# Four edits to the projection of a hybrid attention/recurrence layer: PSUM banks, product order, one engine swap, and a fixed VectorE order

## The chip, the cores and the metric

The kernel runs on one core of a Trainium2 chip. The metric is the device time of one execution in microseconds (us); lower is better. TensorE is called PE, VectorE DVE, ScalarE ACT, GpSimd POOL, and SyncE (which issues the DMAs) SP.

## The reference

One decoder layer on x of shape (1, 1024, 2048), float32:

```
h    = rms_norm(x, norm_gain)
proj = h @ w_in                      # 2048 x 6144: q, k, v, attention gate, recurrent input, recurrent gate
o    = diff_attention(rope(q), rope(k), v, lam)        # 8 heads, two score maps a head, causal
o    = rms_norm(o, subln_gain) * (1 - lam_init) * silu(g_attn)
r    = rg_lru(causal_conv(xr)) * silu(g_rec)           # 8 blocks of 128 channels
out  = rms_norm(x + concat(o, r) @ w_out, final_gain)
...
log_a = -8 * r * softplus(-lru_lambda);  a = exp(log_a)
mult  = sqrt(-expm1(2 * log_a))                        # = sqrt(1 - a*a)
```

## The kernel before

**Products.** All matmuls keep float32 accuracy by splitting each operand into a high and a low part (`hi`, `lo`): three matmuls for one product. The projection is cut into 48 "pairs" of output columns; a pair takes seven block products of a fast matrix scheme (numbers `pi` 0 to 6, 12 matmuls each) over one half (k = 0 or 1) of the contraction. The 48 pairs run in three segments: segment 0 has 8 recurrent pairs of k = 0 (their results go to memory as partials), segment 1 has 16 attention pairs and 8 recurrent pairs of k = 1, segment 2 has the 16 attention pairs of k = 0. In segment 1 the recurrent pairs are finished and `recurrent` follows; in segment 2 the attention pairs are finished and `rope` or `values` follows.

**Banks.** A pair writes its products into four PSUM banks by name, `BANKS = ("al", "de", "be", "al", "ga", "be", "ga")` for `pi` 0 to 6. `post` reads them: after product 0 ACT copies `al`; after 1 DVE makes result 11 from `de`; after 3 ACT copies `al` (L552, called u2) and DVE adds `be` (u3); after 4, 5 and 6 DVE makes results 22, 21 and 12. There are two sets of banks: `pp` (set 0) and `pq` (set 1). The first two pairs of a segment, and the last two of segments 0 and 1, run side by side with one set each; all other pairs run one after another, overlapped, on set 0 alone (`chained`). Of set 1, `al` and `be` also take the small matmuls of `recurrent` and `values`.

**Order.** `projection` writes out the list of products. At each it first writes `prep` of the product three places ahead (for `pi` 2, 3 and 6 a DVE subtraction or two, then `split`; for 4 `split` alone), then the 12 matmuls, then `post`. `split` (L188) is a cast on ACT to `hi` and then a subtraction for `lo`, on DVE, or on POOL for `pi` 0, 1 and 5. Other work (`recurrent`, `rope`, `values`, `scores`, `weighted`) is written as generators that a hand-made clock (`Slots`) advances by four ticks a product, with `yield n` as a delay of n ticks. The order written so is a priority only: the compiler's scheduler orders the instructions of each engine by its own model of when each can start. On the chip each engine then runs its list in that fixed order.

**Later stages.** `rec_half` multiplies the recurrent half by `w_out` (L1097 to L1099) while attention runs (`score` L873 to L910, `unturn` L1018 to L1027). `att_half` then multiplies the attention half; before each of its two row blocks, `att_mix` splits eight operands (cast on ACT, subtraction on DVE), and at its end `finish_row` normalizes.

Of the kernel before, what the change touches and what calls it, by code (L numbers as in the profile page):

```python
# [13 lines left out]
F32 = mybir.dt.float32  # L14
# [3 lines left out]
AF = mybir.ActivationFunctionType  # L18
ALU = mybir.AluOpType
AX = mybir.AxisListType  # L20

P = 128
# [5 lines left out]
NR = 8  # L28
# [25 lines left out]
BANKS = ("al", "de", "be", "al", "ga", "be", "ga")  # L54
# [51 lines left out]
class Pair:  # L106
# [3 lines left out]
    def __init__(self, k, us, done=None, key=None):  # L110
        self.k = k
        self.us = us
        self.done = done
        self.key = key
        self.s = 0
        self.x = {}
        self.w = {}
        self.c = {}
        self.p = {}


class Trunk:
# [86 lines left out]
    def consts2(self):  # L209
        nc, cst, io = self.nc, self.cst, self.io  # L210
        make_identity(nc, self.ident)
        nc.gpsimd.memset(self.mask, 0.0)
        nc.gpsimd.affine_select(
            out=self.mask, in_=self.mask, pattern=[[-1, MASKW]], base=896,
            channel_multiplier=1, compare_op=ALU.is_ge, fill=NEG)
        self.subg = cst.tile([P, 1], F32, name="subg")
        nc.vector.tensor_scalar_mul(self.subg, self.vec[:, VSG:VSG + 1], 0.5 * (1.0 - LAM_INIT))
        b1, b2 = self.alloc(), self.alloc()
        lv = b1.f[:, :4 * QK]
        nc.sync.dma_start(lv, io["lamv"].broadcast_to([P, 4 * QK]))  # L220
        yield 8
        lv = lv.rearrange("p (a b) -> p a b", a=4)
        pr = b2.f[:, :2 * QK].rearrange("p (a b) -> p a b", a=2)
        nc.vector.tensor_tensor(out=pr, in0=lv[:, 0:4:2, :], in1=lv[:, 1:4:2, :], op=ALU.mult)
        sm = cst.tile([P, 2], F32, name="lvs")
        nc.vector.reduce_sum(sm, pr, axis=AX.X)
        self.rel(b1, b2)
        nc.scalar.activation(sm, sm, AF.Exp)
        yield 1
        self.lam = cst.tile([P, 1], F32, name="lam")  # L230
        nc.vector.tensor_tensor(out=self.lam, in0=sm[:, 0:1], in1=sm[:, 1:2], op=ALU.subtract)
        nc.vector.tensor_scalar_add(self.lam, self.lam, LAM_INIT)
        self.nlam = cst.tile([P, 1], F32, name="nlam")
        nc.vector.tensor_scalar_mul(self.nlam, self.lam, -1.0)
        ll = self.vec[:, VLL:VLL + NR]
        t = [cst.tile([P, NR], F32, name=f"sp{i}") for i in range(5)]
        nc.vector.tensor_scalar_mul(t[0], ll, -1.0)
        nc.vector.tensor_tensor(out=t[1], in0=t[0], in1=ll, op=ALU.max)
        nc.scalar.activation(t[1], t[1], AF.Exp, scale=-1.0)
        yield 1  # L240
        nc.vector.tensor_scalar_add(t[2], t[1], 2.0)
        nc.vector.reciprocal(t[2], t[2])
        nc.vector.tensor_tensor(out=t[1], in0=t[1], in1=t[2], op=ALU.mult)
        nc.vector.tensor_tensor(out=t[2], in0=t[1], in1=t[1], op=ALU.mult)
        nc.vector.memset(t[3], 1.0 / 17)
        for k in (15, 13, 11, 9, 7, 5, 3, 1):
            nc.vector.tensor_tensor(out=t[3], in0=t[3], in1=t[2], op=ALU.mult)
            nc.vector.tensor_scalar_add(t[3], t[3], 1.0 / k)
            yield 1
        nc.vector.tensor_tensor(out=t[3], in0=t[3], in1=t[1], op=ALU.mult)  # L250
        nc.vector.tensor_scalar_max(t[4], t[0], 0.0)
        nc.vector.tensor_scalar_mul(t[3], t[3], 2.0)
        nc.vector.tensor_tensor(out=t[4], in0=t[4], in1=t[3], op=ALU.add)
        self.nsp = cst.tile([P, NR], F32, name="nsp")
        nc.vector.tensor_scalar_mul(self.nsp, t[4], -8.0)

# [279 lines left out]
    def partial(self, pr, name):  # L538
        p = pr.p[name] = self.alloc()
        self.load(p.f, self.part[pr.key, name])  # L540

    def post(self, pr, pi):
        nc, b = self.nc, self.bank[pr.s]
        if pi == 0:
            pr.a1 = self.alloc()
            nc.scalar.copy(pr.a1.f, b["al"])
        elif pi == 1:
            self.result(pr, "11", b["de"], pr.a1)
            self.rel(pr.a1)
        elif pi == 3:  # L550
            pr.u2, pr.u3 = self.alloc(), self.alloc()
            nc.scalar.copy(pr.u2.f, b["al"])  # L552
            self.tt(pr.u3.f, b["be"], pr.u2.f, ALU.add)
        elif pi == 4:
            self.result(pr, "22", b["ga"], pr.u3)
            self.rel(pr.u3)
        elif pi == 5:
            self.result(pr, "21", b["be"], pr.u2)
        elif pi == 6:
            self.result(pr, "12", b["ga"], pr.u2)  # L560
            self.rel(pr.u2)
            if pr.done:
                self.after.append(self.sl.spawn(pr.done(pr.c), 1))

    def chained(self, pairs):


        q = [(pairs[0], pi) for pi in range(3)]
        for n, p in enumerate(pairs):
            q += [(p, 3), (p, 4)]  # L570
            for pi in (5, 6):
                if p is not pairs[-1]:
                    q.append((pairs[n + 1], pi - 5))
                q.append((p, pi))
            if p is not pairs[-1]:
                q.append((pairs[n + 1], 2))
        return q

    def projection(self):
        nc, sl = self.nc, self.sl  # L580
# [12 lines left out]
        q, starts, ends, dualp = [], [], [], set()  # L593
# [51 lines left out]
        for i, (p, pi) in enumerate(q):  # L645
            seg = max(s for s in range(3) if starts[s] <= i)
            if i in starts:
                if i == 0:
                    sl.spawn(self.consts2(), 60)
                    sl.spawn(self.squares(sl.spawn(self.second_operands(), 60)), 64)  # L650
                if seg == 1:
                    sl.spawn(self.rope_tables(), 60)
            if seg < 2 and i == ends[seg] - 15:
                sl.spawn(self.operands(1 - seg))
            for x in loads.get(i, ()):
                self.raw(*x)
            for x in parts.get(i, ()):
                self.partial(*x)
            for op in first.pop(i, ()) if seg == 0 else ():
                self.first_operand(op)  # L660
            if i + LEAD < len(q):
                self.prep(*q[i + LEAD])
            if OPS[pi] not in self.Y:
                while len(self.Ynext.get(OPS[pi], ())) < 4:
                    sl.tick()
                self.Y[OPS[pi]] = self.Ynext.pop(OPS[pi])
            dual = p in dualp
            while dual and not self.dual and self.side:
                sl.tick()
            self.dual = dual  # L670
            acc = self.bank[p.s][BANKS[pi]]
            hi, lo = p.w.pop(pi)
            for qq in range(4):
                yh, yl = self.Y[OPS[pi]][qq]
                s = slice(qq * P, (qq + 1) * P)
                for j, (a, b) in enumerate(((hi, yh), (hi, yl), (lo, yh))):
                    nc.tensor.matmul(acc, lhsT=a.r[:, s], rhs=b.r,  # L677
                                     start=FIRST[pi] and qq == 0 and j == 0,
                                     stop=qq == 3 and j == 2, skip_group_check=True)
                sl.tick()  # L680
            self.rel(hi, lo)
            self.post(p, pi)
            if last[seg, pi] == i:
                for hl in self.Y.pop(OPS[pi]):
                    self.rel(*hl)
            if seg == 2 and i >= ends[2] - 7:
                self.out_prefetch(i - ends[2] + 7)
# [15 lines left out]
    def recurrent(self, n, c4):  # L703
        nc, v = self.nc, self.vec
# [48 lines left out]
                yield 2  # L753
            self.rel(ch[l], cl[l])
        self.rel(gw)
        sp = self.nsp[:, n:n + 1]
        th = [self.alloc(), self.alloc()]
        a = [self.alloc(), self.alloc()]
        for l in range(2):
            nc.scalar.activation(th[l].f, gates[l, 0].f, AF.Tanh, scale=sp)  # L760
        for l in range(2):
            nc.scalar.activation(a[l].f, gates[l, 0].f, AF.Exp, scale=sp)
            self.tt(gates[l, 1].f, gates[l, 1].f, cs[l].f, ALU.mult, nc.gpsimd)
            self.rel(cs[l])
            yield 1
        for l in range(2):
            r = gates[l, 0]
            self.tt(r.f, a[l].f, a[l].f, ALU.mult, nc.gpsimd)
            yield 3
            nc.vector.scalar_tensor_tensor(out=r.f, in0=r.f, scalar=1.0, in1=th[l].f,  # L770
                                           op0=ALU.add, op1=ALU.mult)
            yield 1
# [412 lines left out]
            self.rel(y)  # L1185

    def run(self):
        if True:
            self.consts()
            self.projection()  # L1190
            self.rec_half()
            self.att_half()
# [61 lines left out]
```

## Time and profile before

| | |
|---|---|
| median of 3 runs | 1716.01 us (1712.44 to 1718.68) |
| profiled execution | 1710.78 us |
| its span, first to last instruction | 1709.0 us |
| mean granted PE clock | 0.972 |

Most executions of one kernel agree within 0.3%. The busy share of an engine is a mean over stages with different limits; the stages are told apart below by time from the start of the span: the first 214 us hold segment 0, 214 to about 725 us segment 1, to about 1101 us segment 2, 1117 to 1510 us attention beside the first half of the output projection, and the rest the second half.

### The profile page before, as it was taken

How to read it: one execution, taken by the hardware profiler on the slowest of the kernel's cores; microseconds unless marked ns; L12 is line 12 of the kernel's file. 1: busy time of each engine (PE TensorE's matmuls, PEld its weight loads, DVE VectorE, ACT ScalarE, POOL GpSimd, SP SyncE). 2: the span in 40 equal slices, each digit the busy share in tenths (PEclk: the TensorE clock that was granted, in tenths of full speed). 3: DMA queues.
4: the chain of work that ended last, by engine and by line, in shares of the span. 5: the costliest groups of instructions: out<-in, count | busy, mean ns of one | idle time of the engine just before them, and what ended most of it. 6: DMA issues, size and time to landing. Idle time of an engine off the chain costs nothing. (4 is left out here: it accounts for less than half of the span.)

```text
span 1709.0 us, 22289 instructions
## 1 busy us (share of the span) xinstructions
PE 1561.2 (91%) x7140; PEld 1265.1 (74%) x7140; DVE 1278.1 (75%) x2120; ACT 816.4 (48%) x1462; POOL 615.7 (36%) x486
## 2 busy tenths in 40 slices
PE   6977998998999899998998998889999999989997
PEld 4765876787777777877777777767777777868786
DVE  8856759777987889889999988857777777761412
ACT  6443633645456355653323333335665555663432
POOL 3474421424334234451222222324222322357370
PEclk9998999999999999999999999999999999999999
DMA  6665732433424332575665555877577655474642
GB/s 253 223 219 182 240 119 82 130 95 110 131 79 135 120 120 96 196 237 181 205 198 185 183 181 167 298 287 272 177 228 246 209 164 165 147 249 134 223 153 99
DMA packets 168277, 304.18 MB, mean 178 GB/s; under 512 B 19040, under 2 KB 21216, under 8 KB 168160
## 3 DMA queue, kind: packets, MB, share of 16 engines
q1 hardware_dynamic: 168160, 302.76, 53.3%
q8 instruction: 56, 0.92, 0.2%
q14 instruction: 61, 0.50, 0.1%
HBM read 206.22 MB, written 96.47 MB: 177 GB/s over the span
## 5 line engine op out<-in xcount | busy, mean ns | idle before, releaser
L677 PE MATMUL pp<-b,b 128*128 128x512 f32 x3612 | 881.8, 402 | 96.8 <-ACT b L552 49.5
L677 PEld LDWEIGHTS pp<-b,b 128*128 128x128 f32 x3612 | 696.9, 194 | 263.7 <-ACT b L552 57.5
L190 POOL TENSOR_TENSOR b<-b,b 128x512 fp32r<-128x512 f32 x288 | 429.4, 1504 | 779.8 <-ACT b L189 458.1
L189 ACT CAST b<-b 128x512 fp32r<-128x512 f32 x592 | 353.3, 619 | 526.7 <-DVE b L193 202.1
L190 DVE TENSOR_TENSOR b<-b,b 128x512 fp32r<-128x512 f32 x304 | 234.2, 785 | 74.9 <-ACT b L189 52.5
L193 DVE TENSOR_TENSOR b<-b,b 128x512 f32<-128x512 f32 x340 | 269.7, 809 | 18.0 <-DMA b<-w_in 6.3
L1099 PE MATMUL pq<-b,b 128*128 128x512 f32 x512 | 203.3, 397 | 3.6 <-DVE b L190 3.6
L1098 PE MATMUL pq<-b,b 128*128 128x512 f32 x512 | 203.6, 398 | 1.6 <-POOL b L190 1.6
L1097 PE MATMUL pq<-b,b 128*128 128x512 f32 x512 | 203.0, 397 | 0.0
L193 DVE TENSOR_TENSOR b<-pp,b 128x512 f32<-128x512 f32 x215 | 146.1, 680 | 39.3 <-ACT b L552 22.0
L193 DVE TENSOR_TENSOR b<-pq,b 128x512 f32<-128x512 f32 x89 | 61.0, 686 | 108.4 <-PE pq L1099 102.0
L900 ACT ACTIVATE wide<-sw,mx 128x256 f32<-128x256 f32 (+7 forms) x128 | 93.9, 739 | 61.7 <-DVE mx L896 60.4
L193 POOL TENSOR_TENSOR b<-b,b 128x512 f32<-128x512 f32 (+1 forms) x56 | 82.1, 1469 | 106.1 <-DVE b L699 38.3
L1099 PEld LDWEIGHTS pq<-b,b 128*128 128x128 f32 x512 | 96.7, 189 | 21.4 <-DVE b L190 5.4
L193 DVE TENSOR_TENSOR b<-b,wide 128x512 f32<-128x512 f32 x120 | 104.5, 884 | 9.7 <-ACT wide L1167 9.1
L893 DVE CUSTOM_DVE_ANT_0 sw<-sw,mask 128x256 f32<-128x256 f32 (+7 forms) x128 | 96.7, 762 | 17.9 <-PE sw L889 16.4
L1098 PEld LDWEIGHTS pq<-b,b 128*128 128x128 f32 x512 | 96.8, 189 | 17.5 <-POOL b L190 2.0
L1097 PEld LDWEIGHTS pq<-b,b 128*128 128x128 f32 x512 | 96.8, 189 | 15.9
L677 PE MATMUL pq<-b,b 128*128 128x512 f32 x420 | 104.6, 395 | 2.3 <-POOL b L190 1.0
L677 PEld LDWEIGHTS pq<-b,b 128*128 128x128 f32 x420 | 80.1, 191 | 20.3 <-POOL b L190 1.4
L1024 ACT CAST b<-pq 128x512 fp32r<-128x512 f32 (+1 forms) x80 | 43.5, 544 | 76.7 <-PE pq L1015 73.7
L888 PE MATMUL sw<-b,b 128*128 128x512 f32 (+2 forms) x192 | 70.9, 372 | 9.0 <-ACT wide L900 8.7
(149 smaller groups left out, 1574.6 us busy)
## 6 DMA issues: line engine op xcount, KB each, us to landing
b<-w_in SPq DMA_DIRECT2D x192, 256.0 KB, 2.9
b<-w_out SPq DMA_DIRECT2D x128, 256.0 KB, 4.3
pt<-b SPq DMA_DIRECT2D x96, 256.0 KB, 2.7
b<-pt SPq DMA_DIRECT2D x96, 256.0 KB, 2.9
b<-fs SPq DMA_DIRECT2D x96, 256.0 KB, 4.5
b<-xt SPq DMA_DIRECT2D x72, 256.0 KB, 3.9
fs<-b SPq DMA_DIRECT2D x64, 256.0 KB, 2.4
b<-yd SPq DMA_DIRECT2D x32, 256.0 KB, 4.6
```

The lines of the kernel that those rows point to most:

```text
L189: self.nc.scalar.copy(hi.r, x)
L190: (eng or self.nc.vector).tensor_tensor(out=lo.r, in0=x, in1=hi.f, op=ALU.subtract)
L193: (eng or self.nc.vector).tensor_tensor(out=out, in0=a, in1=b, op=op)
L677: nc.tensor.matmul(acc, lhsT=a.r[:, s], rhs=b.r, start=FIRST[pi] and qq == 0 and j == 0, stop=qq == 3 and j == 2, skip_group_check=True)
L888: nc.tensor.matmul(o, lhsT=q[m].r[:, qs], rhs=kk, start=True, stop=False)
L893: nc.vector.tensor_tensor_reduce(out=s, in0=s, in1=self.mask[:, 896 - off:896 - off + cols], scale=1.0, scalar=NEG, op0=ALU.add, op1=ALU.m ...
L900: nc.scalar.activation(p[:, :cols], self.swide[m][:, :cols], AF.Exp, scale=QK ** -0.5, bias=mx[:, m:m + 1], accum_out=sm[:, m:m + 1])
L1024: nc.scalar.copy(wh.r[:, first:], self.tr[:, first:])
L1097: nc.tensor.matmul(acc, lhsT=mh.r[:, s], rhs=wh.r, start=kt == 0, stop=False)
L1098: nc.tensor.matmul(acc, lhsT=mh.r[:, s], rhs=wl.r, start=False, stop=False)
L1099: nc.tensor.matmul(acc, lhsT=ml.r[:, s], rhs=wh.r, start=False, stop=kt == 7)
```

## The change

1. **Banks.** Each second chained pair (`odd`) takes banks `ga` and `de` of set 1 in place of `al` and `be` of set 0; `ga` and `de` of set 0 stay shared by all.
2. **Order.** Products of pair p and the next pair n were written 3p 4p 0n 5p 1n 6p 2n; they are written 3p 4p 0n 1n 5p 6p 2n.
3. **Square.** In `recurrent`, a*a was a POOL multiplication of `a` by itself with a delay of 3 ticks behind it; ACT now makes it as a second Exp of the same input with a doubled scale (`nsp2`), and the delay goes.
4. **DVE order.** The scheduler keeps all DVE instructions in the order in which the program writes them. The other engines are still ordered by the scheduler.

```diff
+        self.nsp2 = cst.tile([P, NR], F32, name="nsp2")
+        nc.vector.tensor_scalar_mul(self.nsp2, t[4], -16.0)
...
+    def banks(self, pr):
+        b = self.bank[pr.s]
+        if pr.odd:
+            b = {**b, "al": self.bank[1]["ga"], "be": self.bank[1]["de"]}
+        return b
+
     def post(self, pr, pi):
-        nc, b = self.nc, self.bank[pr.s]
+        nc, b = self.nc, self.banks(pr)
...
         for n, p in enumerate(pairs):
+            p.odd = n % 2
+            nxt = pairs[n + 1] if p is not pairs[-1] else None
             q += [(p, 3), (p, 4)]
-            for pi in (5, 6):
-                if p is not pairs[-1]:
-                    q.append((pairs[n + 1], pi - 5))
-                q.append((p, pi))
-            if p is not pairs[-1]:
-                q.append((pairs[n + 1], 2))
+            if nxt:
+                q += [(nxt, 0), (nxt, 1)]
+            q += [(p, 5), (p, 6)]
+            if nxt:
+                q.append((nxt, 2))
...
-            acc = self.bank[p.s][BANKS[pi]]
+            acc = self.banks(p)[BANKS[pi]]
...
             nc.scalar.activation(a[l].f, gates[l, 0].f, AF.Exp, scale=sp)
+            nc.scalar.activation(gates[l, 0].f, gates[l, 0].f, AF.Exp, scale=sp2)
...
             r = gates[l, 0]
-            self.tt(r.f, a[l].f, a[l].f, ALU.mult, nc.gpsimd)
-            yield 3
...
     def run(self):
-        if True:
+        with self.tc.manual_schedule(engines={mybir.EngineType.DVE}):
```

## Rows read from the trace of the kernel before

**Rows 1.** The page: busy us, share of the span, instructions of each engine.

```profile
PE 1561.2 (91%) x7140; PEld 1265.1 (74%) x7140; DVE 1278.1 (75%) x2120; ACT 816.4 (48%) x1462; POOL 615.7 (36%) x486
```

**Rows 2.** Stretches: length; busy us (instructions) of each engine; PE clock; DMA share; GB/s.

```profile
85.00:214.00 129.00, 108.78 (x451) 87.60 (x450) 82.86 (x100) 62.63 (x108) 72.29 (x50) 0.93 0.65 213
...
171.00:214.00 43.00, 43.00 (x191) 35.63 (x190) 31.40 (x45) 26.02 (x46) 20.77 (x14) 1.00 0.70 238
...
214.00:725.00 511.00, 473.52 (x2006) 385.35 (x2006) 418.69 (x564) 261.72 (x396) 181.06 (x123) 0.97 0.36 117
...
787.00:1101.00 314.00, 283.93 (x1211) 228.17 (x1210) 291.41 (x416) 107.64 (x187) 78.83 (x47) 0.96 0.62 203
...
1117.00:1510.00 393.00, 367.57 (x2056) 300.79 (x2054) 289.53 (x735) 228.18 (x471) 113.44 (x140) 0.99 0.62 208
```

**Rows 3.** What PE waited for: us in total, times, longest.

```profile
PE pp L677 <- ACT b L552: 49.5, 17, 6.1
PE pp L677 <- DVE b L193: 28.6, 13, 5.4
```

**Rows 4.** What DVE waited for, 787 to 1101 us: total, times, longest.

```profile
DVE b L190 <- ACT b L189: 19.2, 5, 4.6
```

**Rows 5.** The same, 214 to 725 us.

```profile
DVE b L770 <- POOL b L193: 22.5, 6, 7.6
```

**Rows 6.** DVE instructions by form, 787 to 1101 us: busy us, mean ns, idle before.

```profile
L193 DVE TENSOR_TENSOR b<-b,b 128x512 f32<-128x512 f32 x140 | 107.7, 787 | 2.6 <-issue 1.8
L193 DVE TENSOR_TENSOR b<-b,wide 128x512 f32<-128x512 f32 x89 | 79.0, 905 | 0.4
L190 DVE TENSOR_TENSOR b<-b,b 128x512 fp32r<-128x512 f32 x87 | 63.3, 729 | 19.3 <-ACT b L189 19.2
```

**Rows 7.** Timeline around 920 us: start, us, engine, instruction [idle before].

```profile
919.12 0.68 DVE L193 TENSOR_TENSOR b<-b,b 128x512 f32<-128x512 f32 x1
...
919.73 0.68 DVE L193 TENSOR_TENSOR b<-b,wide 128x512 f32<-128x512 f32 x1
919.84 0.62 ACT L189 CAST b<-b 128x512 fp32r<-128x512 f32 x1 [0.58 <-DVE b L193]
920.33 0.68 DVE L193 TENSOR_TENSOR b<-b,b 128x512 f32<-128x512 f32 x1
...
920.93 0.68 DVE L190 TENSOR_TENSOR b<-b,b 128x512 fp32r<-128x512 f32 x1
```

**Rows 8.** Timeline around 308 us, the square and its reader.

```profile
308.17 1.04 POOL L193 TENSOR_TENSOR b<-b 128x512 f32<-128x512 f32 x1 [1.84 <-ACT b L762]
...
309.25 0.69 DVE L770 SCALAR_TENSOR_TENSOR b<-b,b 128x512 f32<-128x512 f32 x1 [6.99 <-POOL b L193]
```

**Rows 9.** Line 193 on DVE: ns minimum/median/maximum by where the inputs lie.

```profile
L193 DVE TENSOR_TENSOR b<-b,b x340: 622/680/1790, 19.2 to 1105.0; 128x512 f32<-128x512 f32 x170
L193 DVE TENSOR_TENSOR b<-pp,b x215: 621/679/693, 23.6 to 1103.2; 128x512 f32<-128x512 f32 x108
```

**Rows 10.** Groups by line: the Exp on ACT, the square on POOL.

```profile
L193 POOL TENSOR_TENSOR b<-b 128x512 f32<-128x512 f32 x16 | 17.0, 1073 | 15.2 <-ACT b L762 8.9 <-ACT b L760 6.2
...
L762 ACT ACTIVATE b<-b,nsp 128x512 f32<-128x512 f32 x16 | 11.6, 722 | 0.1
```

**Rows 11.** Groups by line in attention: Exp of the scores, cast in `unturn`.

```profile
L900 ACT ACTIVATE wide<-sw,mx 128x256 f32<-128x256 f32 (+7 forms) x128 | 93.9, 739 | 61.7 <-DVE mx L896 60.4
...
L900 ACT ACTIVATION_READ_ACCUMULATOR wide<-sw,mx 128x1 f32 x128 | 25.3, 197 | 0.0
...
L1024 ACT CAST b<-pq 128x512 fp32r<-128x512 f32 (+1 forms) x80 | 43.5, 544 | 76.7 <-PE pq L1015 73.7
```

**Rows 12.** DVE timeline at the seam of the last stage's row blocks.

```profile
1605.19 0.69 DVE L190 TENSOR_TENSOR b<-b,b 128x512 fp32r<-128x512 f32 x1 [1.28 <-ACT b L189]
...
1611.05 0.69 DVE L193 TENSOR_TENSOR b<-pq,b 128x512 f32<-128x512 f32 x1 [0.41 <-PE pq L1099]
...
1616.85 0.16 DVE L1178 RECIPROCAL yrs<-yrs 128x1 f32<-128x1 f32 x1 [0.36 <-ACT yrs L1177]
```

More of the change, by code (lines that the diff above doesn't have):

```diff
@@ L119, in __init__ @@
         self.p = {}
+        self.odd = 0
 class Trunk:
@@ L755, in recurrent @@
         self.rel(gw)
-        sp = self.nsp[:, n:n + 1]
+        sp, sp2 = self.nsp[:, n:n + 1], self.nsp2[:, n:n + 1]
         th = [self.alloc(), self.alloc()]
```

## The prediction

> **What bounds the kernel now.** I read the busy line of the page first [rows 1]: PE 91%, DVE 75%. That is an average, so next the stretches [rows 2]. In the projection one stretch shows what PE can do: from 171 to 214 us it ran 191 matmuls in 43.0 us without a gap, 0.225 us each. A pair of seven products is 84 matmuls, 18.9 us. Against this stand three other pictures. From 85 to 214 us PE was busy 108.8 of 129 us at a mean clock of 0.93; from 214 to 725 us 473.5 of 511 at 0.97; from 787 to 1101 us 283.9 of 314 at 0.96. A mean below 1 says that part of the stretch ran at the lower of the two levels, 1.2 in place of 2.4 GHz. In these three stretches PE was idle 20.2, 37.5 and 30.1 us, and the clock shortfall times the length is another 9, 15 and 13 us.
>
> Then I asked what PE waited for [rows 3]. The largest wait is for L552, the ACT copy of bank `al` after product 3: 49.5 us in 17 waits. Product 0 of the next pair writes that same bank, with one product (12 matmuls, 2.7 us) between. The second is for DVE's L193, 28.6 us. So PE's gaps are bank gaps, and the first edit goes for the larger.
>
> The last question is whether the engine behind PE could keep up if those gaps closed. From 787 to 1101 us DVE was busy 291.4 us of 314, 93% [rows 2]: this stage is as much DVE's as PE's. Nearly all that DVE idled there, 19.2 us in 5 waits, was for the cast of `split` [rows 4]. From 214 to 725 us DVE was busy 418.7 of 511, 82% [rows 2], and its largest wait was for the POOL square, 22.5 us in 6 [rows 5]. In attention PE was busy 367.6 of 393 us and DVE 289.5 [rows 2].
>
> **Banks and order.** With its own `al` and `be`, an odd pair's product 0 no longer waits for L552, nor its product 2 for result 21. What is late next is u3, which product 5 needs: with the wider order three products (8.1 us) lie between product 3 and product 5 where there were two. The longest wait for L552 was 6.1 us behind one product [rows 3], so the copy may come 8.8 us after product 3 and still hold up product 5 by about 1.4 us at worst. Shared `ga` keeps its distance: two products between 6 and the next pair's 4. The most the two edits can return is all idle and clock of the three stretches, 20+37+30+9+15+13 = 124 us; the waits for L552 alone are 49.5 us.
>
> The Trainium skill (Perfetto Trace Analysis, Matmuls) says that independent matmul groups should rotate through different PSUM banks, so that one's evacuation overlaps the next one's matmuls. The wait for L552 bears that out; what it gives is a rival below.
>
> **Square.** ACT gains 16 Exp of 722 ns, 11.6 us; POOL loses 16 products of 1073 ns, 17.0 us [rows 10]. ACT is busy 262 of 511 us there [rows 2], so the cover is its idle time; without it, 11.6 us. One example: the square took 1.04 us and its reader on DVE had idled 6.99 us, started 0.04 us after the square's end [rows 8]. The new path is shorter by about 1073 - 722 = 351 ns a half. The dropped ticks and the one extra constant cost nothing that shows beside 48 pairs.
>
> **DVE in the written order.** This is the dear part. In `split`, DVE's subtraction needs ACT's cast, and in `prep` (2, 3 and 6) and `rope` the cast needs the DVE instruction written just before. A piece of the timeline shows the length of that round trip and how it is paid now [rows 7]: a DVE instruction started at 919.12 us, the cast at 919.84 for 0.62, and the subtraction could have started at 920.49 or so. DVE did not stand: it started other instructions at 919.73 and 920.33, and its next subtraction came at 920.93. Kept in written order, nothing can step in, and DVE stands from 919.73 to 920.49, 0.76 us. I count these pairs per stage:
>
> - *787 to 1101 us.* A head has two pairs: 2 x 17 DVE instructions of `prep` and `post`, 16 of `rope`, 8 of `values`: 58. The 416 there [rows 2] are 7.2 heads. A head holds 2 x 3 + 4 = 10 such chains, and two more in `values`, where the subtraction waits for a cast of PE's transposes: 12, or 86 in the stretch. 86 x 0.76 = 65 us, of which 19 are paid now [rows 4]: +46. Some comes back, because a standing DVE does not collide with POOL. Line 193 with both inputs in SBUF takes 622 to 1790 ns, with one from PSUM 621 to 693 [rows 9]; over a median of 680, the three SBUF groups hold (107 x 140 + 225 x 89 + 49 x 87) ns = 39 us of excess [rows 6]. DVE would stand 65 of 356 us, 18%, so I take 7 us of it back: **+39**. Bounds: +7, if all 39 us of excess go; and +46, if none does.
> - *214 to 725 us.* 24 pairs give 72 chains, 55 us; the 16 convolution splits 12; and eight times some 2 us for the first reader of the squares: it is written 2 ticks (1.35 us) behind the Tanh, while ACT needs four activations of 722 ns first [rows 10]. DVE then needs 418.7 + 55 + 12 + 16 = 502 us, less some 10 of collisions. PE needs 24 x 18.9 + 96 x 0.225 = 476 (the last term for `recurrent`'s own matmuls). Both are below the 511 of now, so here the banks may win 19; two engines so near each other do not both run full, and I give half of it back: **-10**. Bounds: -35 (PE's 476), and +26, if half of the 70 us that DVE idles there for other things than the square stays on top of the chains.
> - *85 to 214 us.* 24 chains, 18 us, fit into DVE's 46 idle us [rows 2]. PE has 29 us to win at most, and DMA and POOL, 65% and 56% busy, stay: **-8**, between -20 and +5.
> - *Attention, 64 scores in 393 us, 6.14 each.* DVE is busy 4.52 us a score. Between its maximum and its `es` lie two Exp with their reads, 2 x (739 + 197) = 1.87 us [rows 11], with one instruction of some 0.65 us written in between: 1.2 us of standing; and 1.25 `unturn` a score with a cast of 544 ns [rows 11], half of them early: 0.35. That is 6.07 us, just under 6.14; with no cast early and nothing in between 7.1, or +60 in all. I take **+10**, between 0 and +60.
> - *The last stage's seam.* Now all eight subtractions of the second block's `att_mix` run before the first block's last result (1605.19 against 1611.05). In written order they follow `finish_row`, whose reciprocal came at 1616.85 [rows 12]. PE, which read on at once, would wait some 5 us: **+5**, between +3 and +9.
>
> The Trainium skill (SBUF — State Buffer, Who interferes with whom) has a DVE instruction with two SBUF inputs and a POOL instruction that reads SBUF exclude each other. The spread of line 193 agrees with it; by that rule, with every collision moved into a stand, this stage costs the +7 and the sum is 1715, against 1747 by the rows.
>
> **Sum.** 39 - 10 - 8 + 10 + 5 = +36 us on the profiled 1710.8: 1747. The runs' median is 5 us above that execution, so I put it at **1748**.
>
> **The rivals.**
> - *Banks win* (faster). If DVE's stands cost no more than now in 787 to 1101 us (+7), attention pays nothing, and segments 0 and 1 get most of what the banks can give (-18 and -32): 7 - 18 - 32 + 3 = -40, 1671. For it: the 49.5 us wait is PE's largest and surely goes; the order that is replaced was made from a model, and it lets DVE stand 6.99 us for a POOL product [rows 8]. Against it: the 93% of DVE. It decides if DVE's idle time in 787 to 1101 us stays under 25 us. Chance 0.36. By the rule on banks of the Trainium skill (Perfetto Trace Analysis, Matmuls) the result would be this one.
> - *No change.* The chains cost 20 us and the banks give 20: 1711 to 1721 by either count. Chance 0.09.
> - *Attention breaks too* (much slower). The score chain, not PE, sets its 393 us: +60, with +46 in segment 2, nothing in the two others and +5 at the seam: 1711 + 111 = 1822. For it: 1.55 us a score is all the standing that there is room for. Against it: the output matmuls can fill PE. Chance 0.13.
>
> **How the numbers follow.** My forecast, slower by 15 to 70 us, has 0.42. Within 0.3% (5 us) is about what a measurement of this kernel can tell from no change. Slower is 0.42 + 0.13 = 0.55, same 0.09, faster 0.36. The likeliest case alone spans 1730 to 1785. Both signs are well held, so the range must reach to both rivals: 1650, the faster rival with another 20 us of clock, to 1810; some 0.1 lies outside each end.
>
> **What would show it.** Right: waits for L552 at PE under 15 us; DVE's waits for the cast of `split` at 787 to 1101 us, now 19 us, at 60 or more; that stage, rope's first store to its last, longer than 314 us; the square's wait (22.5 us) gone. Wrong: DVE stands the same or less there while PE's clock rises to 1.00. The step that is likeliest to fail is that a stand is paid in full: if POOL's collisions or PE's gaps hide it, the banks decide.

## The result: 8% slower, and the profile after

The changed kernel takes 1852.21 us (median of 4 runs, 1849.48 to 1854.66) against 1714.22 us before on the same chip (the three runs ahead and one more): a ratio of 1.0804, 95% interval 1.0784 to 1.0823. The forecast was 1748, with 1650 to 1810 as the range. The sign was right; the loss is over four times the forecast one (138 us for 32).

The added lines move the line numbers: L552 (copy of `al`) is now L561, L189 and L190 (cast and subtraction of `split`) are L190 and L191, L193 is L194, L770 (reader of the square) is L779, L677 is L687.

First the busy line of the page, as in [rows 1]:

```profile
PE 1623.1 (88%) x7140; PEld 1267.4 (69%) x7140; DVE 1302.3 (70%) x2121; ACT 826.7 (45%) x1472; POOL 566.6 (31%) x470
```

No engine is busier in share than before. What was added is time in which engines stand. To place it, take events that both programs have, rather than fixed times: first and last store of `rope`, first and last score on DVE. The views by source line of the kernel before, then of the one after (counts, ns minimum/median/maximum, first and last start):

```profile
L820 SPq DMA_DIRECT2D fs<-b x64: 319/320/747, 787.3 to 1101.3; - x64
...
L893 DVE DVE_READ_ACCUMULATOR2_ANT mx<- x128: 132/141/144, 1117.9 to 1510.0; 128x1 f32 x128
```

```profile
L829 SPq DMA_DIRECT2D fs<-b x64: 319/320/939, 835.0 to 1207.4; - x64
...
L902 DVE DVE_READ_ACCUMULATOR2_ANT mx<- x128: 134/142/148, 1217.5 to 1627.8; 128x1 f32 x128
```

| stage, us | before | after | difference |
|---|---|---|---|
| start to the first matmul of `recurrent` | 298.4 | 296.0 | -2 |
| from there to rope's first store | 488.9 | 539.0 | +50 |
| rope's first store to its last | 314.0 | 372.4 | +58 |
| to the first score | 16.6 | 10.1 | -6 |
| first score to the last | 392.1 | 410.3 | +18 |
| last score to the end | 199.0 | 221.5 | +22 |

The two parts of the projection hold 108 of the 140 us. Now the stretches of the changed kernel, cut at these events, to set beside [rows 2]:

```profile
296.00:726.00 430.00, 385.38 (x1569) 293.88 (x1570) 336.91 (x449) 212.95 (x327) 121.93 (x89) 0.98 0.33 107
...
835.00:1207.00 372.00, 308.09 (x1231) 230.85 (x1230) 304.63 (x414) 111.71 (x188) 70.37 (x49) 0.94 0.53 175
1207.00:1217.00 10.00, 8.29 (x39) 6.29 (x37) 6.13 (x7) 2.04 (x4) 4.67 (x3) 1.00 0.91 294
1217.00:1628.00 411.00, 380.48 (x2075) 314.57 (x2073) 297.85 (x744) 233.98 (x479) 117.49 (x143) 0.97 0.61 204
```

From 835 to 1207 us DVE is busy 304.6 us, 82%: less than the 93% of [rows 2]. Read alone, that would say that DVE has room. What it waits for there, and from 296 to 726 us, says otherwise (total, times, longest; compare [rows 4, 5]):

```profile
DVE b L191 <- ACT b L190: 64.8, 85, 1.4
```

```profile
DVE b L191 <- ACT b L190: 53.2, 57, 2.2
DVE b L194 <- ACT b L561: 23.9, 7, 3.8
DVE b L779 <- ACT b L773: 11.4, 4, 3.7
```

304.6 busy and 64.8 standing make 369.4 of 372 us; 336.9 and 88.5 make 425.4 of 430. DVE has no room left in either stretch; it spends the rest of its time waiting for ACT. The timeline shows one turn of this (compare [rows 7]):

```profile
982.73 0.69 DVE L194 TENSOR_TENSOR b<-b,b 128x512 f32<-128x512 f32 x1
983.45 0.62 ACT L190 CAST b<-b 128x512 fp32r<-128x512 f32 x1 [2.69 <-DVE b L194]
...
984.10 0.69 DVE L191 TENSOR_TENSOR b<-b,b 128x512 fp32r<-128x512 f32 x1 [0.68 <-ACT b L190]
```

An instruction, a cast of its result, a subtraction that needs the cast, and 0.68 us in which DVE does nothing. PE in turn waits for what DVE delivers late (compare [rows 3]):

```profile
PE pp L687 <- ACT b L190: 78.6, 43, 10.5
PE pq L687 <- ACT b L190: 20.9, 21, 1.9
PE pq L687 <- DVE b L194: 17.6, 8, 6.2
PE pp L687 <- DVE b L194: 15.9, 16, 1.8
...
PE pq L1108 <- DVE b L191: 8.9, 2, 7.5
```

The 49.5 us for the copy of `al` are gone. In their place stand casts of weights, whose DVE step came late: of the 568 us that ACT idled ahead of its casts, 314 went to a DVE instruction (the page's line; before it was 202 of 527).

```profile
L190 ACT CAST b<-b 128x512 fp32r<-128x512 f32 x592 | 355.6, 619 | 568.3 <-DVE b L194 313.9
```

### The profile page after: what moved, and what is told of

Same layout as the page of the kernel before. It is cut to its first block, busy times and chain, and to the rows that moved or that the text cites. A ratio compares the mean times of both kernels' runs of the same rounds, so it can differ in the third digit from the quotient of the medians.

```text
span 1849.3 us, 22124 instructions
## 1 busy us (share of the span) xinstructions
PE 1623.1 (88%) x7140; PEld 1267.4 (69%) x7140; DVE 1302.3 (70%) x2121; ACT 826.7 (45%) x1472; POOL 566.6 (31%) x470
## 4 chain that ended last, share of the span: by engine, by line
PE 24%; DVE 18%; ACT 5%; issue 5%; DMA 4%; POOL 1%; SPq 1%; ACTq 0%; DVEq 0%; POOLq 0%
DVE b L194 11%; PE pq L1108 5%; PE pq L1106 5%; PE pq L1107 5%; ACT b L190 3%; DVE b L191 2%; PE sw L897 1%; PE pp L687 1%; PE pq L1024 1%; PE sw L898 1%; PE pq L687 1%; DVE sw L902 1%; DMA b<-w_out 1%; ACT wide L909 1%; DMA ys<-b 1%
## 5 line engine op out<-in xcount | busy, mean ns | idle before, releaser
L687 PE MATMUL pp<-b,b 128*128 128x512 f32 x2700 | 694.1, 408 | 100.8 <-ACT b L190 78.6
L687 PEld LDWEIGHTS pp<-b,b 128*128 128x128 f32 x2700 | 514.9, 195 | 259.0 <-ACT b L190 100.9
L191 POOL TENSOR_TENSOR b<-b,b 128x512 fp32r<-128x512 f32 x288 | 404.7, 1417 | 897.4 <-ACT b L190 558.8
L190 ACT CAST b<-b 128x512 fp32r<-128x512 f32 x592 | 355.6, 619 | 568.3 <-DVE b L194 313.9
L687 PE MATMUL pq<-b,b 128*128 128x512 f32 x1332 | 349.3, 403 | 49.4 <-ACT b L190 20.9
L191 DVE TENSOR_TENSOR b<-b,b 128x512 fp32r<-128x512 f32 x304 | 258.1, 862 | 169.7 <-ACT b L190 168.7
L687 PEld LDWEIGHTS pq<-b,b 128*128 128x128 f32 x1332 | 247.5, 191 | 129.2 <-ACT b L190 33.6
L194 DVE TENSOR_TENSOR b<-b,b 128x512 f32<-128x512 f32 x340 | 268.8, 804 | 7.2 <-issue 1.0
L1108 PE MATMUL pq<-b,b 128*128 128x512 f32 x512 | 206.5, 404 | 9.0 <-DVE b L191 8.9
L1106 PE MATMUL pq<-b,b 128*128 128x512 f32 x512 | 208.3, 407 | 5.0 <-DVE b L194 3.2
L1107 PE MATMUL pq<-b,b 128*128 128x512 f32 x512 | 206.6, 403 | 0.5 <-POOL b L191 0.4
L194 DVE TENSOR_TENSOR b<-pq,b 128x512 f32<-128x512 f32 x127 | 87.0, 685 | 150.3 <-PE pq L1108 125.3
L194 POOL TENSOR_TENSOR b<-b,b 128x512 f32<-128x512 f32 (+1 forms) x56 | 76.8, 1372 | 185.2 <-DVE b L709 62.3
L194 DVE TENSOR_TENSOR b<-pp,b 128x512 f32<-128x512 f32 x177 | 120.7, 682 | 18.0 <-ACT b L561 10.4
L1108 PEld LDWEIGHTS pq<-b,b 128*128 128x128 f32 x512 | 98.7, 193 | 28.6 <-DVE b L191 11.9
L1106 PEld LDWEIGHTS pq<-b,b 128*128 128x128 f32 x512 | 98.9, 193 | 24.7 <-DVE b L194 5.5
L1107 PEld LDWEIGHTS pq<-b,b 128*128 128x128 f32 x512 | 98.6, 193 | 17.6 <-POOL b L191 1.3
L194 DVE TENSOR_TENSOR b<-b,wide 128x512 f32<-128x512 f32 x120 | 99.0, 847 | 8.4 <-ACT wide L1176 8.4
```

Of the source, the lines that this page charges most:

```text
L190: self.nc.scalar.copy(hi.r, x)
L191: (eng or self.nc.vector).tensor_tensor(out=lo.r, in0=x, in1=hi.f, op=ALU.subtract)
L194: (eng or self.nc.vector).tensor_tensor(out=out, in0=a, in1=b, op=op)
L687: nc.tensor.matmul(acc, lhsT=a.r[:, s], rhs=b.r, start=FIRST[pi] and qq == 0 and j == 0, stop=qq == 3 and j == 2, skip_group_check=True)
L1106: nc.tensor.matmul(acc, lhsT=mh.r[:, s], rhs=wh.r, start=kt == 0, stop=False)
L1107: nc.tensor.matmul(acc, lhsT=mh.r[:, s], rhs=wl.r, start=False, stop=False)
```

## The experiments

Theory S: in written order DVE pays each wait that the program writes into it, and busy time plus standing is the bound. Each run is given as its median and its ratio to the kernel before, timed on the same chip.

**1. Which edit?** The kernel before with the order alone, and the changed kernel without it:

```diff
 # e1, on the kernel before
-        if True:
+        with self.tc.manual_schedule(engines={mybir.EngineType.DVE}):
 # e2, on the changed kernel
-        with self.tc.manual_schedule(engines={mybir.EngineType.DVE}):
+        if True:
```

> The kernel before with edit 4 alone (DVE in the written order). Theory S (DVE is the bound once it stands for every cast: busy plus standing fills the projection): the order alone carries the loss, and the banks can take little off it, 1840 to 1880 us. Rival R (the new banks and the wider order do the harm, for instance because set 1 is now shared with the small matmuls): close to before, 1710 to 1740 us.

> The changed kernel with edit 4 taken out (banks, order and square stay; DVE scheduled as before). S: PE's waits for L561, the copy of al, nearly vanish and 214 to 725 us gets shorter; the stage from rope's first store to its last stays near 314 us since DVE is 93% busy there: 1670 to 1705 us. R: slower than before, 1730 us or more.

Measured: 1851.88 us for the order alone, ratio 1.0814 (1.0786 to 1.0841), the same as for all four edits; 1697.66 us for the other three, 0.9912 (0.9890 to 0.9934). So the whole loss is the order's, and banks, product order and square are worth 0.9% only where DVE is free. (The scheduler orders the other engines beside the fixed DVE, so their lists may change too; no run tells that share of the loss from DVE's own standing.) With the order alone PE waited only 6.7 us for the copy of `al`, against 49.5 [rows 3]: a PE that DVE holds back everywhere no longer meets the bank, so the banks had nothing left to give. R falls.

Without the written order the stage from rope's first store to its last stays what it was (776 to 1089 us of that run, columns as in [rows 2]):

```profile
776.00:1089.00 313.00, 283.12 (x1212) 228.58 (x1211) 291.63 (x416) 106.84 (x187) 67.58 (x47) 0.96 0.63 204
```

DVE is 93% busy there as before, and no bank helps against that.

**2. Which stage pays?** The changed kernel with the order kept in the projection alone (e3), and in the later stages alone (e11):

```diff
 # e3
         with self.tc.manual_schedule(engines={mybir.EngineType.DVE}):
             self.consts()
             self.projection()
-            self.rec_half()
-            self.att_half()
+        self.rec_half()
+        self.att_half()
 # e11: the other way round
+        self.consts()
+        self.projection()
         with self.tc.manual_schedule(engines={mybir.EngineType.DVE}):
-            self.consts()
-            self.projection()
             self.rec_half()
             self.att_half()
```

> The changed kernel with the written DVE order kept for the constants and the projection alone; attention and the output projection are scheduled freely. S with a cost of its own in each later stage: the projection's 100 us stay, the 38 us behind it go: 1805 to 1825 us. Rival (the later stages are only slow because the projection hands over late or in another state): 1840 to 1855 us.

> The changed kernel with the written DVE order kept for attention and the output projection alone; the projection is scheduled freely. If the stages' costs add (theory S), the 37 us that freeing these stages gave come back on top of 1698: 1730 to 1740 us. Rival (the later stages pay only because the projection hands over in a bad state): 1697 to 1710 us.

Measured: 1814.46 us (ratio 1.0588, 1.0566 to 1.0610) and 1732.21 us (1.0111, 1.0079 to 1.0143). Over the 1697.66 without any order that is 117 and 35 us; together 151, and the full order costs 155. The costs add, so each stage has its own. The later stages of both runs, attention first, then the rest:

```profile
1221.00:1611.00 390.00, 368.29 (x2062) 302.20 (x2061) 286.33 (x735) 227.73 (x470) 113.01 (x140) 0.99 0.64 211
1611.00:1809.00 198.00, 183.85 (x833) 150.16 (x831) 62.00 (x105) 79.72 (x167) 104.77 (x80) 0.99 0.49 168
```

```profile
1101.00:1509.00 408.00, 376.16 (x2071) 309.55 (x2069) 296.88 (x742) 232.48 (x477) 116.59 (x143) 0.98 0.61 203
1509.00:1731.00 222.00, 193.06 (x827) 156.90 (x827) 62.38 (x105) 78.14 (x163) 101.06 (x78) 0.92 0.43 147
```

With the order 18 us more in attention and 24 us more behind it, whatever came before.

**3. Are the stands the price?** Still written order, but the program writes the subtraction later than the cast:

```diff
 # e4: prep is called behind the 12 matmuls, four products ahead, and returns its subtraction
-            if i + LEAD < len(q):
-                self.prep(*q[i + LEAD])
...
+            rest = self.prep(*q[i + 1 + LEAD], late=True)
             self.post(p, pi)
+            if rest:
+                rest()
 # rope and convolution: subtraction a tick behind the cast
-            self.split(t1.f, t2, t1)
+            self.split_late(t1.f, t2, t1)
```

> The changed kernel, still in written DVE order, but the program writes DVE's subtraction of a split later than its cast: in prep behind the results of the product that has just been written, in rope and in the convolution a tick later. S: most of the 191 us that DVE stood for the cast in the projection go, and the stage from rope's first store to its last falls from 372 to 320 or 335 us: 1750 to 1790 us in all. Rival T (weights come too late because the program prepares only three products ahead, and DVE's stands just fill that time): no gain, 1835 to 1860 us.

Measured: 1808.17 us, 1.0557 (1.0537 to 1.0577): 44 us off, short of the 60 to 100 that I expected. Rope's stage took 350.7 us (817.8 to 1168.5), 21.7 less, where 320 to 335 us were expected. The run's waits of DVE (L539 is the subtraction of `prep`, L194 and L198 those of the two forms of `split`, L202 the helper for additions, L577 the copy of `al`), whole run:

```profile
DVE b L202 <- ACT b L577: 57.8, 15, 8.8
DVE b L539 <- ACT b L536: 55.8, 67, 2.8
DVE b L194 <- ACT b L193: 48.4, 35, 7.6
...
DVE b L198 <- ACT b L197: 21.7, 30, 1.3
```

For casts DVE still stood 126 us, where the changed kernel stood 194 us in 208 waits over the whole run: a third went, not most of it. For the copy of `al` it stood 58 in place of 32. Net 43 us less standing, and 44 us less time: about one for one. That is S in its price; its count of what the edit would remove was too high. T falls in its strict form. This kernel also calls `prep` ahead of the `post` behind which it stood, so part of the gain could be that; no run has it alone. Experiment 5 tests a longer lead by itself, in free order.

Then the addition for u3, which waits for that copy, was written two ticks later as well (e12):

```diff
-            self.tt(pr.u3.f, b["be"], pr.u2.f, ALU.add)
+            self.sl.late.append((self.sl.now + 2, lambda: self.tt(
+                pr.u3.f, b["be"], pr.u2.f, ALU.add)))
```

> The run with the subtractions written later, and u3 (DVE's addition behind the ACT copy of al) written two ticks later as well. Theory S (DVE pays for each wait that the program writes into its order, whatever it waits for): of the 58 us that DVE stood for that copy there, 30 to 45 go, and the time falls by 20 to 45 us from 1808: 1763 to 1788 us. Rival (the copy is late because ACT is, and DVE only meets the wait elsewhere): within 10 us of 1808.

Measured: 1799.69 us (1795.48 to 1808.23), 1.0509 (1.0466 to 1.0551). The wait only fell from 57.8 to 49.9 us. S's expectation was missed and the rival's fits: the copy itself is late. In the changed kernel ACT ran without a gap up to one such copy (ACT's timeline; DVE idled 3.80 us for it):

```profile
498.81 1.27 ACT L761 ACTIVATE b<-pq,vec 128x512 f32<-128x512 f32 x2
500.00 0.62 ACT L190 CAST b<-b 128x512 fp32r<-128x512 f32 x1
500.53 0.72 ACT L770 ACTIVATE b<-b,nsp 128x512 f32<-128x512 f32 x1
501.16 0.56 ACT L561 COPY b<-pp 128x512 f32<-128x512 f32 x1
```

Two sigmoids, a cast and a Tanh of `recurrent` stand ahead of it. That these cause all such waits was not tested.

**4. Do the stands spare collisions with POOL?** The forecast took 7 us back for that. To measure it, POOL's subtraction in `prep` was left out of both kernels; the high part stands in for the low part of products 0, 1 and 5.

```diff
-        hi, lo = self.allocr(), self.allocr()
-        self.split(src.f, hi, lo, eng)
+        hi = self.allocr()
+        if pi in POOL_LO:
+            self.nc.scalar.copy(hi.r, src.f)
+            lo = ...   # the same buffer as hi
```

> The changed kernel without POOL's subtraction in prep (products 0, 1 and 5): the high part stands in for the low part there, so the output is not the layer's; PE's, DVE's and ACT's instructions stay. Theory C (POOL's operations slip into DVE's stands and then hold up the subtraction behind the stand, so that collisions cost more in written order than before): the stage from rope's first store to its last falls from 372 to 335 us or less, DVE's mean for a subtraction of a split from 790 to about 690 ns, 1760 to 1800 us in all. Rival (the subtraction got longer for another reason): less than 15 us.

> The kernel before without POOL's subtraction in prep (products 0, 1 and 5; the high part stands in for the low part, so the output is not the layer's). C: collisions cost the kernel before less than the changed one, since PE and DVE share the bound there: 20 to 45 us faster than before, 1670 to 1693 us. Rival: as much as or more than the changed kernel gains by the same cut.

Measured: 1780.55 us, ratio to before 1.0390 (1.0363 to 1.0417), from the changed kernel; 1625.21 us, 0.9483 (0.9454 to 0.9512), from the one before. C falls in its claim that the written order pays more: the cut is worth 72 us there, and 89 before, where C had 20 to 45. For the changed kernel without the subtractions, the stretch from rope's first store to its last (columns as in [rows 2]), and then DVE's groups in it:

```profile
800.00:1146.00 346.00, 304.39 (x1241) 232.49 (x1239) 272.52 (x414) 114.16 (x191) 14.58 (x11) 0.96 0.59 194
```

```profile
L194 DVE TENSOR_TENSOR b<-b,wide 128x512 f32<-128x512 f32 x90 | 62.9, 727 | 0.0
L191 DVE TENSOR_TENSOR b<-b,b 128x512 fp32r<-128x512 f32 x87 | 60.4, 695 | 52.8 <-ACT b L190 51.7 <-DMA b<-pt 1.1
```

The same two views of the kernel before without them:

```profile
734.00:1013.00 279.00, 276.82 (x1248) 228.99 (x1247) 260.39 (x417) 109.68 (x188) 8.36 (x7) 1.00 0.68 227
```

```profile
L193 DVE TENSOR_TENSOR b<-b,b 128x512 f32<-128x512 f32 x141 | 95.0, 694 | 4.0 <-DMA vs<-b 3.2 <-DMA fs<-b 0.3
L193 DVE TENSOR_TENSOR b<-b,wide 128x512 f32<-128x512 f32 x89 | 61.1, 690 | 0.9 <-DMA gs<-b 0.2
L190 DVE TENSOR_TENSOR b<-b,b 128x512 fp32r<-128x512 f32 x87 | 59.5, 696 | 8.5 <-DMA vs<-b 4.8 <-ACT b L189 3.6
```

DVE's busy time falls by 291.4 - 260.4 = 31 us before and by 304.6 - 272.5 = 32 after: collisions cost DVE the same in both, so the stands spared nothing in this stage. The pair says more. Without POOL's subtractions the stretch takes 278 us in free order, where PE is busy 276.8 of 279 at a clock of 1.00, and 346 in written order. Of the 67 us between, 55 are DVE standing longer (73.5 us of idle time, 68.9 of it for casts, against 18.6) and 12 its longer busy time.

**5. The three other edits, and the lead.** In free DVE order: banks and product order alone (e5), square alone (e6), and all three with `LEAD = 4` in place of 3 (e8).

```diff
 # e5, on e2: back to the product on POOL
-            nc.scalar.activation(gates[l, 0].f, gates[l, 0].f, AF.Exp, scale=sp2)
...
+            self.tt(r.f, a[l].f, a[l].f, ALU.mult, nc.gpsimd)
+            yield 3
 # e6: the old banks and the old product order, with the square on ACT
 # e8, on e2
-LEAD = 3
+LEAD = 4
```

> The kernel before with banks and wider order alone (POOL's square kept, DVE scheduled freely). Theory S (the 49.5 us that PE waited for the copy of al are what the two edits give back): most of the 16 us gain of the run without the written order, 1698 to 1706 us. Rival Q (that gain came from the square, whose reader cost DVE 22.5 us of waiting): 1711 to 1718 us.

> The kernel before with the square by ACT alone. S: PE did not wait for the square, so nothing that can be measured, 1708 to 1716 us. Q: 1697 to 1705 us.

> The changed kernel without the written DVE order, and with weights prepared four products ahead in place of three. S (where DVE is 93% busy the lead does not matter, and elsewhere PE's 20 us of waits for the cast are at the opening): 1692 to 1700 us. Rival T (weights come too late): 1675 to 1690 us.

Measured: 1708.38 us, 0.9980 (0.9965 to 0.9995); 1706.41 us, 0.9976 (0.9961 to 0.9991); 1696.54 us, 0.9908 (0.9885 to 0.9931). Each alone gives 0.2%, which the intervals barely tell from nothing, together 0.9%; both S's and Q's sharp forms fall, and why the two help each other stays open. The lead is worth nothing that can be told here.

**6. The seam.** The changed kernel with the second block's `att_mix` written ahead of the first block's last four results:

```diff
             for h in range(8):
-                self.att_mix(h, b)
+                if b == 0:
+                    self.att_mix(h, b)
...
                     self.load(y.f, self.ysc[b, cg, t])
+                    if b == 0 and cg == 3 and t == 0:
+                        for h in range(8):
+                            self.att_mix(h, 1)
```

> The changed kernel, written DVE order and all, but the program writes the second row block's att_mix ahead of the first block's last four results. S (at the seam PE waits because eight subtractions are written behind finish_row): the longest wait of L1108 for DVE, 7.5 us, and the low clock behind it go, 8 to 13 us faster than the changed kernel: 1839 to 1845 us. Rival (the seam waits for the loads): within 4 us of 1852.

Measured: 1846.95 us, ratio to before 1.0797 (1.0772 to 1.0823), which the changed kernel's 1.0804 can't be told from; the 1839 to 1845 us expected were missed. In its place the edit worked: PE's waits for L191 behind the last score fell from 8.9 to 1.8 us (those for L194 rose from 0.6 to 4.9), and from the last score to the end it was 213.4 us in place of 221.5. But the last score came 4.5 us later than in the changed kernel, so the whole shows no gain.

## Why the prediction was right in sign and wrong in size

- **Banks and order.** The wait for L552 went, as said. The forecast did not see that the written order alone already takes it to 6.7 us, so that in the changed kernel the banks give nothing. The Trainium skill's rule on rotating banks (Perfetto Trace Analysis, Matmuls) holds for the wait; banks and product order gave 0.2% in time by themselves. My first rival rested on it and falls: even in free order the three edits gave 16 us, not its 40.
- **A stand's price.** 0.76 us and 86 chains, 65 us from 787 to 1101 us; measured 64.8 us in 85 waits. Right, though this was the step that the forecast doubted most.
- **Rope's stage, +39, measured +58.** The stands are +46 as forecast. The failed term is the 7 us taken back for collisions: DVE's busy time grew, 291.4 to 304.6 us. Without POOL's subtractions it grew as much, 260.4 to 272.5, so POOL is not why. Count times mean, added up over DVE's groups by form in the stretch, is 322.1 us before and 324.0 after: the instructions hardly got longer. Busy time counts once what two instructions overlap, and 11 of the 13 us are overlap that went. A DVE instruction of 0.68 us is followed by the next 0.60 us after its start [rows 7]; a stand undoes that overlap of 0.08, by estimate about 7 us in 85. The other 4 stay open.
- **Segment 1, -10, measured +37.** Where a segment begins can be read from PE's timeline: the last two pairs of one and the first two of the next run side by side, 28 products that alternate between `pp` and `pq`, and the 15th of them is the new segment's first. For segments 1 and 2 that was this product, before and then after:

```profile
204.29 2.88 PE L677 MATMUL pp<-b,b 128*128 128x512 f32 x12
...
743.02 2.88 PE L677 MATMUL pp<-b,b 128*128 128x512 f32 x12
```

```profile
212.56 2.88 PE L687 MATMUL pp<-b,b 128*128 128x512 f32 x12
...
788.10 2.89 PE L687 MATMUL pp<-b,b 128*128 128x512 f32 x12
```

  So segment 1 lasted from 204 to 743 us before, not from 214 to 725 as said ahead, and took 538.7 us; it takes 575.5 now, for 2118 and 2117 recorded matmuls. Its stretch before, its stretch after (columns as in [rows 2]), and what DVE waited for in the second:

```profile
204.29:743.02 538.73, 499.43 (x2118) 406.18 (x2116) 442.60 (x592) 276.47 (x421) 198.82 (x135) 0.97 0.38 123
```

```profile
212.56:788.10 575.54, 518.58 (x2117) 395.67 (x2116) 445.66 (x594) 281.86 (x437) 169.14 (x121) 0.98 0.37 117
```

```profile
DVE b L191 <- ACT b L190: 75.8, 76, 4.2
DVE b L194 <- ACT b L561: 24.9, 10, 3.8
DVE b L779 <- ACT b L773: 15.0, 6, 3.7
```

  This is the step that failed most: "Both are below the 511 of now, so here the banks may win 19". The cast chains were sized nearly well (67 forecast, 75.8 measured), the reader of the square too (16 forecast, 15.0). But the sum took 10 us back for collisions, where DVE's busy time rose by 3; it left out DVE's wait for the copy of `al` (24.9 us, the u3 that I named as late next without pricing it; 10.7 before); and it had no place for DVE's other idle time (14 us). Busy and these three waits are 561 us, more than the whole segment took before, and the +37 lies outside the bound of +26.
- **Segment 0, -8, measured +8**, by the first products of segment 1 above: 204.3 us before, 212.6 after. The loss is in the opening, for which the sum had no term. In the first 85 us DVE stood 25.1 us for casts (2.3 before), and PE waited 27.8 us for casts (11.5 before) and ran 213 matmuls in place of 266:

```profile
0.00:85.00 85.00, 69.39 (x266) 52.87 (x267) 74.45 (x130) 45.17 (x80) 32.89 (x24) 0.98 0.70 239
```

```profile
0.00:85.00 85.00, 56.94 (x213) 43.56 (x214) 56.16 (x83) 41.87 (x70) 18.05 (x19) 0.88 0.59 202
```

  In the rest of the segment, the stretch that was forecast, PE did win: 461 matmuls in 127.6 us, 3.6 a us, where it had run 408 in 119.3, 3.4 a us.
- **Attention, +10, measured +18.** Within the bounds of 0 to +60. The two things that were priced, 99 us in all, were the Exp (62.5 us, 45.8 before) and the casts of `unturn` (19.0, 12.8 before). DVE stood for one more that was not: the chain of `head_out` (12.7, 1.7 before).
- **The seam, +5.** In experiment 6 the stretch behind the last score was 8 us shorter, near the upper bound of +9; how much of that is the seam alone is not shown. But this stretch cost 22: the entry into the last stage was not thought of. From 1628 to 1660 us PE was busy 20.7 of 32 us at a clock of 0.68, where in the first 32 us behind the last score before it was busy 27.1 at 1.00. Which of the waits there is the cause was not tried.
- **The square.** The 22.5 us wait did not go: its reader waits 15.0 us, now for ACT's Exp. With DVE scheduled freely (e2) 0.5 us of it is left.
- **The sum.** It adds up to 36 us. On the runs' median of 1716 that is 1752, not the 1748 put down; the difference changes nothing here.

So the mechanism was right: DVE pays its stands in full. The size was not: the measured 138 us lie above the 15 to 70 of the main case (0.42) and above the 111 of the third case. The errors are terms left out or taken back, all in one direction. The third case had attention as the place of a large loss; it was the projection.

## What to carry to other kernels

An engine's busy share is not its load once its order is fixed: add the time that it stands for others. When a program writes a value's consumer right behind a round trip to another engine, fixing that order charges every round trip in full, here 194 us in 208 waits for casts; so count such pairs and compare busy plus standing with the stage's length before fixing an order. And undo one edit of a bundle before judging the rest: three of these four make the kernel 0.9% faster, 1697.66 us, and that is the version to keep.

## What the runs showed of the hardware that was not expected

Cutting POOL's subtractions in `prep`, and with them the low part of products 0, 1 and 5, took the kernel before down 5.2%, more than any scheduling edit. DVE's means for two SBUF inputs fell from 787 to 694, from 905 to 690 and from 729 to 696 ns [rows 6]. The Trainium skill (SBUF — State Buffer, Who interferes with whom) says that such DVE instructions and POOL's reads of SBUF exclude each other; the spread of 622 to 1790 ns [rows 9] and this cut agree with it. What does not follow is that a DVE that stands more collides less: in rope's stage 31 us of busy time with few stands, 32 with many.
